# Tables and layer 0's parameter rows loaded in the last piece; ScalarE alone normalizes x; bias rows turned first

## The chip, the core and the metric

The kernel runs on one core of a Trainium2 chip. TensorE (PE), VectorE (DVE), ScalarE (ACT) and GpSimd (POOL) each run a queue of instructions in order; SyncE (SP) issues nearly all DMAs, and POOL issues a few. The metric is the device time of one execution in microseconds (us): the median of 3 runs. A difference of 0.2% (4.6 us) is about what a measurement of this kernel can tell from no change.

## The reference

A trunk of two layers on x, 256 positions by 2048 channels, float32, with a condition vector c. Each layer makes six modulation vectors from c, projects the modulated normalized input into four groups of heads, puts them together, and ends with a gated feed-forward network. The part that the change touches is the start of layer 0:

```python
c_act = jax.nn.silu(c)
mod = (c_act @ w_mod[l] + b_mod[l]).reshape(bn, 6, d)
shift_m, scale_m, gate_m = mod[:, 0, None], mod[:, 1, None], mod[:, 2, None]
h = layer_norm(x) * (1.0 + scale_m) + shift_m
proj = h @ w_in[l]
...
y_b = mla_mixer(..., cos, sin)          # rotary tables
y_d = conformer_conv(ag, conf_w_dw[l], conf_b_dw[l], conf_ln_g[l], conf_ln_b[l])
...
gate = causal_dwconv(gate, w_conv, b_conv)   # in the feed-forward part
```

`w_mod` has 2048 x 12288 numbers a layer (100 MB), so even the two vectors that the first products need, `shift_m` and `scale_m`, take 33.5 MB of weights.

## The kernel before

**Pieces.** Layer 0 cannot wait until all of `shift_m` and `scale_m` is there, so `by_pieces` (L1248) goes through the 2048 input channels in five pieces, `PIECES` (L45): 2, 2, 4, 4 and 4 blocks of 128 channels, called pieces 0 to 4 here. For a piece, `mod_piece` (L251) loads the columns of `w_mod` that make its channels' shift and scale, in units of 1 MB (two DMAs of 512 KB, one for each of the two vectors, tile `wmod`). DVE multiplies each k-block by c's value and adds it up in `qacc` (`mod_step`, L243, its lines L246 and L248). `sums` (L275) lets PE add `qacc` over the partitions (`ps_mod`, L83) on top of the bias, which PE takes from `bcol`, a tile with `b_mod` turned so that channels lie on partitions; ACT writes the result as columns (`mod`, L205 and L86). Then `finish` (L1474) multiplies and shifts the piece's normalized x, `hF`: even blocks on ACT, odd ones on DVE (L1484). From piece 2 on `hF` is also split into a high and a low part, `hT` (L473, L474). PE now adds the piece's share of five groups of products, D, U, V, B and E, into PSUM or into running sums (`sumU` and others, L1280, L1292).

**Order.** A scheduler lays each engine's queue out at build time, and each engine then runs its queue in that order. While piece q is multiplied, the units of piece q+1 are loaded and added up (L1327 to L1342), and `finish` of piece q+1 is called ahead of the last quarter of piece q's D products. SP's queue holds the `wmod` units and the projection's weights (`wexact`, 512 KB or 384 KB; `wraw`, 1 MB, which ACT and DVE split into `whi` L453 and `wlo` L454) interleaved. A transfer can be issued only when its buffer is free: `wmod` and `wraw` share four 1 MB buffers, `wexact` eight buffers of 512 KB. `wmod` buffers are freed by DVE's `qacc` instructions, `wexact` buffers by PE.

**x.** `normed_T` (L1442) loads x's two tiles of 128 positions. DVE takes the statistics (L1449, L569, L571), POOL the power to -0.5 (L114), and DVE the product -mean * rstd (L574). ACT writes the normalized quarter `xn` (L86), PE turns it (`ps_xT`, L1456), and the copy into `hF` goes to ACT for quarters 0 and 2 (L1460) and to DVE for quarters 1 and 3 (L1462).

**Rows.** Small parameters come as rows of 128 numbers and are turned by PE. `load_rows` (L130) lets POOL load them (L135) into one of five buffers and returns a `turn`: a PE transpose (`ps_rows`, L141) and a DVE copy (L142). At the start POOL loads `b_mod` of layer 0, the tables `cst[:, 128:1024]` (rotary tables and small matrices, L157), and the rows of `load_params(0)` (L167): ten DMAs for four turns, `pm` (conformer weights; norms and other small ones) and `pf` (feed-forward convolution, two turns). `turn_b0` stands in `finish` of piece 0 (L1476), the four others in `finish` of piece 1 (L1487 to L1490). POOL then loads the same five sets of rows for layer 1 as soon as the five buffers are free again.

After piece 4, the rest of group B and then C follow (`B_c`, `C_c`), while DVE and ACT work on group D's convolution (`gluD`, `convD`, `prodD`), on A's mixing (`va`, `wT`, `ps_mix`) and on attention (`mix_b`, L1023), which needs the tables, `pm` and `rr` (`ps_ss`, `ps_rkv`, `dgB`).

Of the kernel before, what the change touches and what calls it, by code (L numbers as in the profile page):

```python
# [13 lines left out]
P = 128  # L14
# [40 lines left out]
def encoder_kernel(ctx: ExitStack, tc: tile.TileContext, A: dict, consts: bass.AP, out: bass.AP):  # L55
# [71 lines left out]
    cact = keep.tile([P, 16], F32, name="cact")  # L127
    dve.tensor_copy(cact, pst[:, 0:16])

    def load_rows(parts, n, dst):  # L130

        r = smallp.tile([P, P], F32, tag="rows", name="rows", bufs=5)
        at = 0
        for ap in parts:
            pool.dma_start(out=r[at : at + ap.shape[0], :], in_=ap)  # L135
            at += ap.shape[0]
        assert at == n

        def turn():
            ps = ms_tile("ps_rows")  # L140
            pe.transpose(ps[:, 0:n], r[0:n, :], ident[0:n, 0:n])  # L141
            dve.tensor_copy(dst, ps[:, 0:n])  # L142
# [12 lines left out]
    turn_b0 = load_rows([rows(A["b_mod"][0])], 96, bcol[0])

    pool.dma_start(out=cst[:, 128:1024], in_=consts[:, 128:1024])  # L157

    PM = []
    PF = []  # L160
# [1087 lines left out]
    def by_pieces(l, w_in, hF, between, mix_d, mix_u, mix_v, mix_b, mix_c, mix_e):  # L1248
# [52 lines left out]
        for q, (k0, nkt) in enumerate(PIECES):  # L1301
# [140 lines left out]
    def normed_T(hF):  # L1442
# [3 lines left out]
        for t in range(2):  # L1446
            st = new_stats(f"in{t}")
            for c in range(4):
                dve.bn_stats(out=st[:, c, :], in_=X[t][:, c * 512 : (c + 1) * 512])  # L1449
            r = rstd_of(st, f"in{t}", True)[1]  # L1450
            for q in range(4):
                xn = tmp_tile("xn")
                ident_act(xn, X[t][:, q * 512 : (q + 1) * 512], r[:, 0:1], r[:, 1:2])
                ps = ms_tile("ps_xT")
                for j in range(4):
                    pe.transpose(ps[:, j * P : (j + 1) * P], xn[:, j * P : (j + 1) * P], ident)  # L1456
                dst = hF[q][:, :, t * P : (t + 1) * P]
                src = ps.rearrange("p (j t) -> p j t", j=4)
                if q % 2 == 0:
                    act.copy(dst, src)  # L1460
                else:
                    dve.tensor_copy(dst, src)  # L1462

    def piece(q, hF):

        k0, nkt = PIECES[q]
        units, sums = mod_piece(0, (SHIFT_M, SCALE_M), k0, nkt)
        if q == 0:
            normed_T(hF)
            for u in units:  # L1470
                u()
            turns.extend(load_params(0))

        def finish():  # L1474
            if q == 0:
                turn_b0()  # L1476
            sums()
            for kt in range(k0, k0 + nkt):
                h = hF[kt // 4][:, kt % 4, :]
# [1 line left out]
                if kt % 2 == 0:  # L1481
                    ident_act(h, h, sc, sh)
                else:
                    dve.tensor_scalar(out=h, in0=h, scalar1=sc, scalar2=sh, op0=ALU.mult, op1=ALU.add)  # L1484
            for kt in range(max(k0, PLAIN_KT), k0 + nkt, 2):
                split(hT[kt // 2], hF[kt // 4][:, kt % 4 : kt % 4 + 2, :])
            if q == 1:  # L1487
                for turn in turns:
                    turn()
                turns.clear()  # L1490
# [123 lines left out]
```

## Time and profile before

| what | value |
|---|---|
| runs | 2288.36, 2288.9, 2292.54 us; median 2288.9 us |
| profiled execution | 2287.06 us, its span 2285.3 us |
| PE busy in the span | 2233.5 us (98%) |
| DVE, ACT, POOL busy | 1773.9, 1095.1, 33.7 us |
| DMA | 605.21 MB, mean 265 GB/s |
| granted TensorE clock, mean | 0.991 |

The span runs from the first to the last instruction of the profiled execution; 1.8 us of that execution's time lie around it. Rows of the timeline give the start and the length of a run of like instructions, their engine, line, output and inputs, and in brackets how long the engine sat idle before and what ended that. Rows of the windows give the busy time of PE, its weight loads, DVE, ACT and POOL in a stretch, then the granted clock, the mean busy share of the 16 DMA engines (a saturated stretch reads a little over 1) and GB/s.

### The profile page before, as it was taken

To read this page: it belongs to the slowest core of one execution; us is meant where nothing else is said; L and a number is where in the kernel's file an instruction comes from. 1 tells how busy PE (TensorE), PEld (TensorE's weight loads), DVE (VectorE), ACT (ScalarE), POOL (GpSimd) and SP (SyncE) were. 2 spreads that over 40 slices of the span, in tenths; PEclk is the share of its full clock that TensorE was granted. 3 is DMA by queue.
4 is the path that set the end of the run, shared out by engine and by line. 5 is a ranking of instruction groups with operands and counts; after the bars stand their busy time and mean duration, and the time that the engine had idled before them with its cause. 6 is when DMAs were issued, how large, how long until landed. Compare 5 with 4: busy or idle time off the path is not lost.

```text
span 2285.3 us, 31502 instructions
## 1 busy us (share of the span) xinstructions
PE 2233.5 (98%) x12387; PEld 1929.9 (84%) x12387; DVE 1773.9 (78%) x2187; ACT 1095.1 (48%) x1638; POOL 33.7 (1%) x65
## 2 busy tenths in 40 slices
PE   6999999999999999999999999999999999999998
PEld 4788886798888888888789999889888888888886
DVE  5768988788888888988977899787676565565776
ACT  3346741354455444544454434545544454454553
POOL 1000000000000000000000000000000000000000
PEclk9999999999999999999999999999999999999999
DMA  9999789778888888898767667775666555555554
GB/s 350 371 364 354 276 310 360 249 277 315 310 310 313 314 303 329 301 345 305 276 221 260 197 237 251 275 272 188 239 240 206 200 183 192 195 186 191 187 193 148
DMA packets 228717, 605.21 MB, mean 265 GB/s; under 512 B 14660, under 2 KB 27188, under 8 KB 210900
## 3 DMA queue, kind: packets, MB, share of 16 engines
q1 hardware_dynamic: 227784, 602.30, 74.2%
q8 instruction: 97, 1.59, 0.3%
q0 software_dynamic: 784, 0.90, 0.1%
q14 instruction: 52, 0.43, 0.0%
HBM read 601.05 MB, written 2.10 MB: 264 GB/s over the span
## 4 chain that ended last, share of the span: by engine, by line
PE 53%; DVE 4%; DMA 1%; issue 1%; ACT 1%; POOL 0%; DVEq 0%; POOLq 0%; ACTq 0%
PE d L83 20%; PE v_c L83 12%; PE g_c L83 11%; PE o L83 2%; PE D_c L83 2%; PE C_c L83 2%; PE U_c L83 1%; DVE wlo L454 1%; DVE convD L886 1%; PE E_c L83 1%; DMA wmod<-in_w_mod_dram 1%; DMA wraw<-in_w_out_dram 1%; DVE macc L248 0%; PE ps_mod L83 0%; PE ps_xT L592 0%
## 5 line engine op out<-in xcount | busy, mean ns | idle before, releaser
L453 ACT CAST whi<-wraw 128x1024 fp32r<-128x1024 f32 (+1 forms) x632 | 643.3, 1043 | 750.0 <-PE g_c L83 221.5
L454 DVE TENSOR_TENSOR wlo<-wraw,whi 128x1024 fp32r<-128x1024 f32 (+1 forms) x632 | 750.1, 1214 | 298.9 <-ACT whi L453 276.6
L83 PE MATMUL d<-whi,a 128*128 128x512 f32 x1344 | 390.4, 391 | 0.9 <-ACT whi L453 0.9
L248 DVE SCALAR_TENSOR_TENSOR macc<-wmod,cact,macc 128x2048 f32<-128x2048 f32 (+2 forms) x174 | 353.6, 2033 | 41.3 <-DMA wmod<-in_w_mod_dram 40.7
L83 PE MATMUL v_c<-hT,whi 128*128 128x512 f32 (+1 forms) x1456 | 343.1, 383 | 0.0
L83 PE MATMUL g_c<-hT,whi 128*128 128x512 f32 (+1 forms) x1344 | 313.6, 380 | 1.3 <-DVE second L1429 1.3
L83 PEld LDWEIGHTS v_c<-hT,whi 128*128 128x128 f32 x1456 | 264.5, 189 | 48.5
L83 PEld LDWEIGHTS d<-whi,a 128*128 128x128 f32 x1344 | 253.4, 189 | 54.6 <-ACT whi L453 2.2
L83 PEld LDWEIGHTS g_c<-hT,whi 128*128 128x128 f32 x1344 | 243.4, 189 | 44.9 <-DVE second L1429 1.8
L83 PE MATMUL d<-wlo,a 128*128 128x512 f32 x672 | 235.1, 393 | 1.6 <-DVE wlo L454 1.6
L83 PE MATMUL v_c<-hT,wlo 128*128 128x256 f32 x1400 | 190.7, 283 | 0.0
L83 PEld LDWEIGHTS v_c<-hT,wlo 128*128 128x128 f32 x1400 | 183.1, 191 | 6.6
L83 PE MATMUL g_c<-hT,wlo 128*128 128x256 f32 x1280 | 175.8, 283 | 0.0
L83 PEld LDWEIGHTS g_c<-hT,wlo 128*128 128x128 f32 x1280 | 168.2, 191 | 5.9
L83 PEld LDWEIGHTS d<-wlo,a 128*128 128x128 f32 x672 | 127.1, 189 | 30.2 <-DVE wlo L454 3.8
L473 ACT CAST a<-g 128x512 fp32r<-128x512 f32 x132 | 80.7, 619 | 91.8 <-PE d L83 90.0
L83 PE MATMUL o<-whi,a 128*128 128x512 f32 x384 | 110.1, 392 | 0.5 <-ACT whi L453 0.5
L474 DVE TENSOR_TENSOR a<-g,a 128x512 fp32r<-128x512 f32 x132 | 87.6, 683 | 10.2 <-ACT a L473 10.2
L248 DVE SCALAR_TENSOR_TENSOR qacc<-wmod,cact,qacc 128x1024 f32<-128x1024 f32 (+1 forms) x75 | 80.3, 1070 | 10.5 <-DMA wmod<-in_w_mod_dram 8.4
L83 PEld LDWEIGHTS o<-whi,a 128*128 128x128 f32 x384 | 71.9, 188 | 16.6 <-ACT whi L453 0.9
L83 PE MATMUL D_c<-hT,whi 128*128 128x256 f32 x432 | 83.1, 292 | 2.4 <-ACT hT L473 1.6
L83 PEld LDWEIGHTS D_c<-hT,whi 128*128 128x128 f32 x432 | 69.8, 197 | 4.8 <-ACT hT L473 1.7
(370 smaller groups left out, 2605.9 us busy)
## 6 DMA issues: line engine op xcount, KB each, us to landing
wraw<-in_ffn_w_up_dram SPq DMA_DIRECT2D x168, 1024.0 KB, 5.0
wmod<-in_w_mod_dram SPq DMA_DIRECT2D x134, 1024.0 KB, 6.7
wraw<-in_ffn_w_down_dram SPq DMA_DIRECT2D x88, 1024.0 KB, 5.2
wraw<-in_w_in_dram SPq DMA_DIRECT2D x33, 1024.0 KB, 6.6
wmod<-in_w_mod_dram SPq DMA_DIRECT2D x64, 512.0 KB, 9.5
wraw<-in_w_out_dram SPq DMA_DIRECT2D x26, 1024.0 KB, 6.9
wmod<-in_w_mod_dram SPq DMA_DIRECT2D x32, 768.0 KB, 7.4
wexact<-in_w_in_dram SPq DMA_DIRECT2D x46, 512.0 KB, 8.0
```

Source lines behind the costliest of these rows:

```text
L83: pe.matmul(o, lhsT, rhs, start=start, stop=stop, skip_group_check=True)
L248: i = dve.scalar_tensor_tensor(out=acc, in0=w, scalar=col, in1=acc, op0=ALU.mult, op1=ALU.add)
L453: act.copy(hi[:, :m], r)
L454: i = dve.tensor_tensor(out=lo[:, :m], in0=r, in1=hi[:, :m].bitcast(F32), op=ALU.subtract)
L473: act.copy(hi, src)
L474: dve.tensor_tensor(out=lo, in0=src, in1=hi.bitcast(F32), op=ALU.subtract)
L886: dve.scalar_tensor_tensor(out=yd[:, j, 30 - k :], in0=glu[:, j, : S - 30 + k], scalar=CW(k, j), in1=yd[:, j, 30 - k :], op0=ALU.mult, op1 ...
```

## The change

Four things are edited.

1. `turn_b0` moves from `finish` of piece 0 to a place ahead of `normed_T`: `b_mod`'s rows are turned first.
2. `normed_T` no longer uses `rstd_of`. DVE writes var + eps and -mean; POOL takes the power; ACT makes -mean * rstd by a Copy of -mean with rstd as its scale. All eight turned quarters are copied into `hF` by ACT.
3. The tables' DMA and the rows of `load_params(0)` are issued in `finish` of piece 4, with a dependency (a semaphore) on the last DVE instruction that modulates `hF` there.
4. Their four turns are called during piece 4's products: one after V, one after E, two after the last quarter of D. The `next(mods)` calls there are as before.

```diff
     turn_b0 = load_rows([rows(A["b_mod"][0])], 96, bcol[0])
-
-    pool.dma_start(out=cst[:, 128:1024], in_=consts[:, 128:1024])
...
-                if k0 + nkt == KT and s < 3:
-                    next(mods)
+                if k0 + nkt == KT:
+                    if s < 3:
+                        next(mods)
+                    if s > 0:
+                        turns.pop(0)()
+                    if s == 3:
+                        turns.pop(0)()
...
-            r = rstd_of(st, f"in{t}", True)[1]
+            mv = smallp.tile([P, 2], F32, tag="mv", name=f"mv_in{t}", bufs=4)
+            dve.bn_aggr(out=mv, in_=st)
+            r = smallp.tile([P, 3], F32, tag="rin", name=f"r_in{t}")
+            dve.tensor_scalar(out=r[:, 0:1], in0=mv[:, 1:2], scalar1=LN_EPS, scalar2=None, op0=ALU.add)
+            dve.tensor_scalar(out=r[:, 2:3], in0=mv[:, 0:1], scalar1=-1.0, scalar2=None, op0=ALU.mult)
+            power(r[:, 0:1], r[:, 0:1])
+            act.activation(out=r[:, 1:2], in_=r[:, 2:3], func=AF.Copy, scale=r[:, 0:1])
...
-                dst = hF[q][:, :, t * P : (t + 1) * P]
-                src = ps.rearrange("p (j t) -> p j t", j=4)
-                if q % 2 == 0:
-                    act.copy(dst, src)
-                else:
-                    dve.tensor_copy(dst, src)
+                act.copy(hF[q][:, :, t * P : (t + 1) * P], ps.rearrange("p (j t) -> p j t", j=4))
...
         if q == 0:
+            turn_b0()
             normed_T(hF)
             for u in units:
                 u()
-            turns.extend(load_params(0))
...
-                    dve.tensor_scalar(out=h, in0=h, scalar1=sc, scalar2=sh, op0=ALU.mult, op1=ALU.add)
+                    i = dve.tensor_scalar(out=h, in0=h, scalar1=sc, scalar2=sh, op0=ALU.mult, op1=ALU.add)
+            if q + 1 == len(PIECES):
+                d = pool.dma_start(out=cst[:, 128:1024], in_=consts[:, 128:1024])
+                tc.add_manual_dep(d.ins, i.ins.name, data_dep, reason="the pieces' weights go first")
+                turns.extend(load_params(0, i))
```

(`load_params` and `load_rows` pass the instruction on and add the same dependency to each row DMA.)

DVE's queue at the start of layer 0, before: `st_in`, `mv_in` and `rs_in` are the norms' small columns, `qacc` piece 0's sums, `hF` the turned x.

```order
L571 TENSOR_SCALAR rs_in1_187<-mv_in1_185 128x1
L246 TENSOR_SCALAR qacc_134<-wmod_223,cact_104 128x512
L248 SCALAR_TENSOR_TENSOR qacc_134<-wmod_223,cact_104,qacc_134 128x512 x2
L574 SCALAR_TENSOR_TENSOR rs_in0_144<-mv_in0_142,rs_in0_144 128x1
L574 SCALAR_TENSOR_TENSOR rs_in1_187<-mv_in1_185,rs_in1_187 128x1
L248 SCALAR_TENSOR_TENSOR qacc_134<-wmod_223,cact_104,qacc_134 128x512
L248 SCALAR_TENSOR_TENSOR qacc_134<-wmod_230,cact_104,qacc_134 128x512 x3
L1462 COPY hF1_116<-ps_xT_158 128x4x128
L248 SCALAR_TENSOR_TENSOR qacc_134<-wmod_230,cact_104,qacc_134 128x512
L1462 COPY hF3_118<-ps_xT_174 128x4x128
L248 SCALAR_TENSOR_TENSOR qacc_134<-wmod_237,cact_104,qacc_134 128x512
L1462 COPY hF1_116<-ps_xT_201 128x4x128
```

The same place with the change (`bcol` is the turned bias, `r_in` the norm's columns):

```order
L144 COPY bcol0_106<-ps_rows_134 128x96
L1456 BN_STATS st_in0_139<-x0_97 128x6 x4
L1458 BN_AGGR mv_in0_144<-st_in0_139 128x2
L1460 TENSOR_SCALAR r_in0_146<-mv_in0_144 128x1
L1461 TENSOR_SCALAR r_in0_146<-mv_in0_144 128x1
L1456 BN_STATS st_in1_183<-x1_98 128x6 x4
L1458 BN_AGGR mv_in1_188<-st_in1_183 128x2
L1460 TENSOR_SCALAR r_in1_190<-mv_in1_188 128x1
L1461 TENSOR_SCALAR r_in1_190<-mv_in1_188 128x1
L248 TENSOR_SCALAR qacc_133<-wmod_227,cact_104 128x512
L250 SCALAR_TENSOR_TENSOR qacc_133<-wmod_227,cact_104,qacc_133 128x512 x3
L250 SCALAR_TENSOR_TENSOR qacc_133<-wmod_234,cact_104,qacc_133 128x512 x4
```

The four copies into `hF` and the two products for the norm are gone from between the sums, the copy of the bias (before, four `qacc` ahead of the end of piece 0's sums) stands ahead of x's statistics, and piece 0's sixteen `qacc` instructions stand in one run.

DVE's queue in the products of piece 4, before (`wlo`: low parts of weights, `macc`: sums for a later modulation vector, `gluD`: the first step behind group D, `wT`: A's mixing weights, turned):

```order
L474 TENSOR_TENSOR hT<-hF_118,hT 128x2x256 x2
L246 TENSOR_SCALAR macc<-wmod,cact 128x2048
L454 TENSOR_TENSOR wlo<-wraw,whi 128x1024 x3
L248 SCALAR_TENSOR_TENSOR macc<-wmod,cact,macc 128x2048
L454 TENSOR_TENSOR wlo<-wraw,whi 128x1024 x4
L248 SCALAR_TENSOR_TENSOR macc<-wmod,cact,macc 128x2048
L454 TENSOR_TENSOR wlo<-wraw,whi 128x1024
L248 SCALAR_TENSOR_TENSOR macc<-wmod,cact,macc 128x2048 x2
L875 TENSOR_TENSOR gluD<-D_c_119,sg 128x512
L875 TENSOR_TENSOR gluD<-D_c_120,sg 128x512
L987 COPY wT<-ps_wT 128x512
```

And with the change (`pm`, `pf`: the turned parameters):

```order
L456 TENSOR_TENSOR wlo<-wraw,whi 128x1024 x3
L250 SCALAR_TENSOR_TENSOR macc<-wmod,cact,macc 128x2048
L456 TENSOR_TENSOR wlo<-wraw,whi 128x1024 x4
L144 COPY pm_110<-ps_rows 128x124
L456 TENSOR_TENSOR wlo<-wraw,whi 128x1024
L250 SCALAR_TENSOR_TENSOR macc<-wmod,cact,macc 128x2048 x2
L144 COPY pm_110<-ps_rows 128x29
L250 SCALAR_TENSOR_TENSOR macc<-wmod,cact,macc 128x2048
L144 COPY pf_111<-ps_rows 128x128
L144 COPY pf_111<-ps_rows 128x48
L877 TENSOR_TENSOR gluD<-D_c_118,sg 128x512
L877 TENSOR_TENSOR gluD<-D_c_119,sg 128x512
```

The four copies, which stood in piece 2's `qacc` run before, are now here, two of them right ahead of `gluD`, and one `macc` has gone back behind a `wlo`.

POOL's queue around the two powers, before (`rows_260` and `rows_262` are the last two of layer 0's row sets, `rows_2737` the first of layer 1's):

```order
L135 DMA rows_260<-in_ffn_w_conv_dram 128x128
L135 DMA rows_262<-in_ffn_w_conv_dram 4x128
L135 DMA rows_262<-in_ffn_b_conv_dram 44x128
L114 ISA
L114 TENSOR_TENSOR rs_in0_144<-rs_in0_144,mhalf_93 128x1
L114 TENSOR_TENSOR rs_in1_187<-rs_in1_187,mhalf_93 128x1
L135 DMA rows_2737<-in_b_mod_dram 96x128
```

And with the change (`rows_108` is layer 0's bias, `cst` the tables, `rows_1021` and `rows_1023` the first of layer 0's other sets):

```order
L135 DMA rows_108<-in_b_mod_dram 96x128
L104 MEMSET flat_84 128x1 x4
L114 ISA
L114 TENSOR_TENSOR r_in0_146<-r_in0_146,mhalf_93 128x1
L114 TENSOR_TENSOR r_in1_190<-r_in1_190,mhalf_93 128x1
L1492 DMA cst_82<-in_consts_dram 128x896
L135 DMA rows_1021<-in_conf_w_dw_dram 124x128
L135 DMA rows_1023<-in_mla_q_norm_dram 3x128
```

The powers stand ahead of the tables and of all rows but the bias; layer 1's loads follow behind layer 0's, ahead of the clearing of `wT` as before.

More of the change, by code (lines that the diff above doesn't have):

```diff
@@ L128, in encoder_kernel, with load_rows @@
     dve.tensor_copy(cact, pst[:, 0:16])
-    def load_rows(parts, n, dst):
+    def load_rows(parts, n, dst, behind=None):
         r = smallp.tile([P, P], F32, tag="rows", name="rows", bufs=5)
@@ L134, in load_rows @@
         for ap in parts:
-            pool.dma_start(out=r[at : at + ap.shape[0], :], in_=ap)
+            i = pool.dma_start(out=r[at : at + ap.shape[0], :], in_=ap)
+            if behind is not None:
+                tc.add_manual_dep(i.ins, behind.ins.name, data_dep, reason="the pieces' weights go first")
             at += ap.shape[0]
@@ L149, in rows @@
         return ap.rearrange("k (j p) -> (k j) p", p=P)
+    order_dep = mybir.DependencyInfo(mybir.DependencyClass.NoSync, mybir.DependencyReason.DATA)
+    data_dep = mybir.DependencyInfo(mybir.DependencyClass.Sync, mybir.DependencyReason.DATA)
     bcol = []
@@ L165, in encoder_kernel, with load_params @@
         PF.append(pf)
-    def load_params(l):
+    def load_params(l, behind=None):
         turns = []
         if l > 0:
-            turns.append(load_rows([rows(A["b_mod"][l])], 96, bcol[l]))
-        turns.append(load_rows([rows(A["conf_w_dw"][l])], 124, PM[l][:, 0:124]))
+            turns.append(load_rows([rows(A["b_mod"][l])], 96, bcol[l], behind))
+        turns.append(load_rows([rows(A["conf_w_dw"][l])], 124, PM[l][:, 0:124], behind))
         turns.append(
@@ L183, in load_params @@
                 PM[l][:, 124:153],
+                behind,
             )
@@ L186, in load_params @@
         wc = rows(A["ffn_w_conv"][l])
-        turns.append(load_rows([wc[0:128]], 128, PF[l][:, 0:128]))
-        turns.append(load_rows([wc[128:132], rows(A["ffn_b_conv"][l])], 48, PF[l][:, 128:176]))
+        turns.append(load_rows([wc[0:128]], 128, PF[l][:, 0:128], behind))
+        turns.append(load_rows([wc[128:132], rows(A["ffn_b_conv"][l])], 48, PF[l][:, 128:176], behind))
         return turns
     MOD, MOD_BY = {}, {}
-    order_dep = mybir.DependencyInfo(mybir.DependencyClass.NoSync, mybir.DependencyReason.DATA)
-    data_dep = mybir.DependencyInfo(mybir.DependencyClass.Sync, mybir.DependencyReason.DATA)
     def mod_cols(l, m, k0, acc):
@@ L1471, in piece @@
                 u()
-            turns.extend(load_params(0))
         def finish():
-            if q == 0:
-                turn_b0()
             sums()
@@ L1483, in finish @@
                 else:
-                    dve.tensor_scalar(out=h, in0=h, scalar1=sc, scalar2=sh, op0=ALU.mult, op1=ALU.add)
+                    i = dve.tensor_scalar(out=h, in0=h, scalar1=sc, scalar2=sh, op0=ALU.mult, op1=ALU.add)
[3 more added lines that the diff above has]
+                turns.extend(load_params(0, i))
             for kt in range(max(k0, PLAIN_KT), k0 + nkt, 2):
                 split(hT[kt // 2], hF[kt // 4][:, kt % 4 : kt % 4 + 2, :])
[L1487 to L1490, printed above, removed]
         return ([] if q == 0 else units), finish
```

## The prediction

> **What bounds the kernel now.** I read the head of the page first: what the span holds, and whose work fills it.
>
> ```profile
> span 2285.3 us, 31502 instructions
> PE 2233.5 (98%) x12387; PEld 1929.9 (84%) x12387; DVE 1773.9 (78%) x2187; ACT 1095.1 (48%) x1638; POOL 33.7 (1%) x65
> ```
>
> PE does 2233.5 us of 2285.3. What the change can save lies in the other 52 us, most of it at the start, and it is kept only if what feeds PE later can follow. So I cut the start into stretches (columns: stretch, its length, busy PE, PEld, DVE, ACT, POOL, granted clock, DMA share, GB/s).
>
> ```profile
> 5.00:22.00 17.00, 3.95 (x17) 3.26 (x18) 12.09 (x23) 5.23 (x8) 4.22 (x8) 1.00 1.06 364
> 22.00:40.00 18.00, 13.25 (x59) 11.01 (x58) 14.95 (x23) 3.68 (x8) 0.59 (x1) 0.81 1.08 362
> 40.00:58.00 18.00, 18.00 (x82) 14.20 (x80) 6.19 (x10) 7.09 (x14) 0.00 (x0) 1.00 1.05 390
> 58.00:62.00 4.00, 4.00 (x19) 3.31 (x19) 3.96 (x7) 0.10 (x1) 3.77 (x8) 1.00 0.54 145
> 62.00:70.00 8.00, 7.98 (x39) 6.73 (x38) 7.79 (x7) 1.59 (x3) 1.31 (x3) 1.00 1.02 366
> 70.00:130.00 60.00, 56.91 (x296) 46.83 (x297) 43.31 (x42) 26.18 (x46) 0.00 (x0) 0.94 1.04 391
> ```
>
> The transfers are saturated (share over 1) from 5 to 130 us but for one hole, 58 to 62 (0.54, 145 GB/s). PE idles until about 33 us and is full behind that but for small gaps. Two limits therefore lie over each other: when PE can begin, and when bytes arrive. The timelines of PE and DVE show the first, and where the two meet.
>
> ```profile
> 7.28 2.47 DVE L1449 BATCH_NORM_STATS2 st_in<-x 128x6 f32<-128x512 f32 x4 [2.46 <-DMA x<-in_x_dram]
> 11.36 2.47 DVE L1449 BATCH_NORM_STATS2 st_in<-x 128x6 f32<-128x512 f32 x4 [1.12 <-DMA x<-in_x_dram]
> 14.61 0.49 DVE L246 TENSOR_SCALAR qacc<-wmod,cact 128x512 f32<-128x512 f32 x1 [0.29 <-DMA wmod<-in_w_mod_dram]
> 27.16 3.11 DVE L248 SCALAR_TENSOR_TENSOR qacc<-wmod,cact,qacc 128x512 f32<-128x512 f32 x4
> 33.18 5.16 PE L83 MATMUL D_c<-hF,wexact 128*128 128x256 f32 x16
> 55.85 0.95 PE L83 MATMUL ps_mod<-onesR,qacc 128*128 128x1 f32 x8
> 57.13 0.41 DVE L1484 TENSOR_SCALAR hF<-hF,mod,mod 128x256 f32<-128x256 f32 x1 [5.45 <-ACT mod L86]
> 70.38 3.67 PE L83 MATMUL V<-wexact,hF 128*128 128x512 f32 x8 [0.39 <-DMA wexact<-in_w_in_dram]
> ```
>
> Piece 0's sums end on DVE at 30.27 (27.16 + 3.11); 2.9 us later (reduction on PE, `mod`, `hF`) D starts, at 33.18. From there PE runs to 70.38, where V of piece 1 waits 0.39 us for its weights. That is the first place where PE catches up with the transfers: a gain at the start has to pass it.
>
> **The start, on the engines.** What one instruction costs, by the groups of the first 33 us (count | busy us, mean ns | idle before):
>
> ```profile
> L248 DVE SCALAR_TENSOR_TENSOR qacc<-wmod,cact,qacc 128x512 f32<-128x512 f32 x15 | 11.2, 748 | 0.8 <-DMA wmod<-in_w_mod_dram 0.5
> L86 ACT ACTIVATE xn<-x,rs_in 128x512 f32<-128x512 f32 x8 | 6.1, 809 | 12.5 <-DVE rs_in L574 12.5
> L1462 DVE COPY hF<-ps_xT 128x512 f32<-128x512 f32 x4 | 2.8, 688 | 0.8 <-PE ps_xT L1456 0.8
> L1460 ACT COPY hF<-ps_xT 128x512 f32<-128x512 f32 x4 | 2.3, 575 | 0.8 <-PE ps_xT L1456 0.8
> L142 DVE COPY bcol<-ps_rows 128x96 f32<-128x96 f32 x1 | 0.2, 250 | 0.0
> ```
>
> Sixteen sums take 0.49 + 15 x 0.748 = 11.7 us; before, they took 14.61 to 30.27 = 15.7, with 2.8 of copies, 0.25 of `bcol` and two short products among them. Now they stand in one run, and two bounds hold. By DVE: x's second tile should land some 1.4 us sooner, since the tables and rows (0.63 MB at 364 GB/s are 1.7 us) no longer share its transfer time; DVE starts the sums at 13.2 and ends at 24.9. By bytes: behind the first x tile (7.28) come 1 MB of x and eight transfers of 0.52 MB, 5.2 MB or 14.4 us at 364 GB/s, so the last unit is in at 21.7 to 22; four sums behind it (3.0) end at 24.7 to 25. Both say 25.0: 5.3 us sooner, D at 27.9.
>
> ACT now does 8 x (0.809 + 0.575) = 11.1 us, two tiny products besides. From the first norm (7.28 + 2.47 of statistics, short columns and POOL's power: about 11) and with a wait for the second tile it ends at 22 to 23.5. PE needs these columns at 27.9, ACT itself is wanted for `mod` at about 26: the cover is 2.5 us or more, so the move costs nothing; with a cover gone each further 1.4 us of ACT would count in full. The bias turn on PE and its 0.25 us copy now stand ahead of x on DVE; DVE was idle there for 2.46 us, so nothing.
>
> **What leaves the boundary of piece 2.** The four turns stand between D products there:
>
> ```profile
> 57.60 0.44 PE L141 MATMUL ps_rows<-cst,rows 124*128 124x124 f32 x2
> 58.51 0.47 PE L141 MATMUL ps_rows<-cst,rows 128*128 128x128 f32 x2
> SPq L263 <- DVE pf L142: 9.0, 1, 9.0
> ```
>
> PE gets back 0.8 us (0.44 + 0.47, less overlap), and is 6.1 us ahead. The last row is from SP's waits: one `wmod` issue stood 9.0 us until DVE had come past its modulation of piece 1 (57.13) and the turns' copies; that made the hole. With DVE let through at about 52, buffers come free at about 53 to 54, before the earlier issues run out (at 58, or 56 with fewer bytes ahead): the hole should close.
>
> **How far the transfers follow.** Ahead of V's weights no longer come the tables 0.46, layer 0's rows 0.17 and, while piece 0 runs, layer 1's `b_mod` 0.05 MB: 0.68 MB / 0.363 = 1.9 us. The hole gives (390 - 145) x 4 us = 0.98 MB, 2.5 us. Layer 1's rows, in 62 to 70 us: (391 - 366) x 8 = 0.2 MB, 0.5 us. Together 4.9 us. So PE, 6.1 ahead, waits 1.2 us more at V than before and goes on 4.9 ahead; behind that the transfers stay at 1.04, so no more comes until 130 us. The 0.8 of the turns and some of the start are lost in this wait.
>
> **Piece 4.** POOL loads once DVE has modulated there:
>
> ```profile
> 158.18 0.74 DVE L1484 TENSOR_SCALAR hF<-hF,mod,mod 128x256 f32<-128x256 f32 x2 [0.86 <-ACT mod L86]
> 177.54 0.40 PE L83 MATMUL D_c<-hT,whi 128*128 128x256 f32 x2
> rows<-in_conf_w_dw_dram POOLq DMA_DIRECT2D x2, 62.0 KB, 5.3
> 140.00:185.00 45.00, 45.00 (x293) 39.67 (x292) 29.38 (x25) 25.96 (x37) 0.00 (x0) 1.00 0.92 328
> 4.32 0.50 POOL L135 DMA_DIRECT2D rows<-in_sconv_w_dram  x1
> 59.75 0.50 POOL L135 DMA_DIRECT2D rows<-in_sconv_w_dram  x1
> ```
>
> DVE's second modulation ends at 158.9, now 154.0. The tables and ten row loads at 0.5 us are issued by 160, and rows land 5.3 us later, by 166. The first turn stands behind V, at 177.54, now 172.6; the others later: no wait, 6 us and more of cover. On PE the turns cost again 0.8 us, as at their old place: 4.9 - 0.8 = 4.1.
>
> On DVE the four copies cost about 1.1 us; two come right ahead of `gluD`, in a stretch that this view of DVE shows:
>
> ```profile
> 188.58 2.35 DVE L248 SCALAR_TENSOR_TENSOR macc<-wmod,cact,macc 128x2048 f32<-128x2048 f32 x1 [4.40 <-DMA wmod<-in_w_mod_dram]
> 190.84 1.28 DVE L875 TENSOR_TENSOR gluD<-D_c,sg 128x512 f32<-128x512 f32 x2
> 204.19 1.10 DVE L1009 TENSOR_TENSOR mixed<-ps_mix,gmlp 128x256 f32<-128x256 f32 x3 [0.59 <-PE ps_mix L83]
> 226.12 1.70 PE L83 MATMUL ps_ss<-onesR,sqB 128*128 128x1 f32 x12 [0.98 <-ACT sqB L1045]
> 235.34 0.67 PE L83 MATMUL ps_rkv<-dgB,onesR 128*128 128x256 f32 x2 [0.76 <-DVE dgB L1074]
> ```
>
> DVE waits 4.40 us for the last `macc`; the first two copies go into such idle. The last two delay `gluD` by some 0.65, and 0.59 of idle at 204.19 takes most of that back. PE waits for this chain at 226.12 and 235.34, 1.74 us in all: bounds of this term are +0.8 (all copies arrive there) and -1.7 (both waits go, since the new order has a `convD` step less ahead of `dgB`'s column). I take +0.1 (0.65 - 0.59), the rows nearest to `gluD`. The 0.63 MB beside the weights of piece 4 cost nothing: from 140 to 185 us, 328 GB/s run where 391 is full, room for 2.8 MB. Without it they would put off that last `macc` by 1.6 us (0.63 / 0.391), which `gluD` would feel.
>
> **Sum.** -4.9 + 0.8 + 0.1 = -4.0. The profiled span 2285.3 becomes 2281.3, its execution 2287.06 becomes 2283.1. That execution lies 1.8 us below the median of the runs, 2288.9; I carry the difference over to the median: 2284.9.
>
> **The rivals.** One measurement of this kernel tells 0.2%, 4.6 us, from no change: faster is below 2284.3. The forecast stands at the edge of it.
>
> *A, the forecast*: -4.0, 2284.9; chance 0.45.
>
> *B, the hole stays*: `wmod` buffers come free late after all, since the sums of piece 1 wait for their own units. Then bytes give 2.4, less 0.9: -1.5, 2287.4. Against it: DVE idled 5.45 us ahead of 57.13, so it was done with those sums. Chance 0.12.
>
> *C, the longer stall at V turns the clock down.* PE waits 1.6 us there where it waited 0.39. Other waits of that length, and the clock in a stretch behind them:
>
> ```profile
> 87.00 0.98 PE L83 MATMUL D_c<-hT,whi 128*128 128x256 f32 x4 [1.62 <-ACT hT L473]
> 93.00:94.00 1.00, 1.00 (x7) 1.00 (x7) 1.00 (x1) 0.00 (x0) 0.00 (x0) 0.50 1.06 391
> 226.00:228.00 2.00, 1.88 (x13) 1.88 (x14) 2.00 (x4) 1.57 (x5) 0.00 (x0) 0.82 0.99 416
> 228.00:230.00 2.00, 2.00 (x6) 1.55 (x6) 2.00 (x3) 2.00 (x7) 0.00 (x0) 0.50 1.01 418
> ```
>
> After 1.62 us of idle at 87 and 0.98 at 226 the granted clock was 0.50. Half a clock over about 3.4 us (an estimate: 228 to 230 is wholly at 0.50, 226 to 228 at 0.82 holds 0.7 us of it, and as much again is taken for the far edge) loses 1.7: -2.3, 2286.6. Chance 0.18. [...]
>
> *D, more than forecast*: the waits of 226.12 and 235.34 go, up to 1.74, and with the first the half clock behind it, 1.7: -5.7 to -7.4 if all goes, -4.0 if nothing; I put it at -6.0, 2282.9. For it: the shorter DVE order ahead of `dgB`. Against: two copies more ahead of `gluD`. Chance 0.20.
>
> *E, the slower side: POOL's issues drag in piece 4.* If an issue takes long while DVE is busy, the last turn's rows come too late, and PE, which runs in order, stands at the turn with C's and B's products queued behind it. From 154.0 to the last turn (about 184, an estimate between the end of V, 172.6, and `gluD`, 190.84 - 4.9) less 5.3 of landing are 25 us for 11 issues: it decides from 2.3 us an issue. [...] Against it: an issue took 0.50 us at 59.75, where DVE was 99% busy, as at 4.32. [...] Chance 0.05.
>
> **How the numbers follow.** C, B and A's upper bounds (+0.8 for `gluD`, +1.6 for a late `macc`) reach to 2287.4, and the highest cases together with some of the runs' own spread to 2288.6; D and the lower bounds reach to 2280.8, which leaves out E and part of D's far end. Faster by over 0.2%: D and nearly half of A, 0.41; slower: E, 0.05; within: the rest, 0.54.
>
> **What would show it.** Right: D of piece 0 at 27.9; DVE's sums from 13.2 to 25.0 without a gap of note; ACT's last copy before 25; no stretch near 58 under 350 GB/s; a wait of 1 to 2 us at V of piece 1; no wait at any of the four turns; the end of V in piece 4 4.9 us earlier, the last product 4.0. Wrong: D begins after 29 (ACT, or bytes); V does not wait and PE is 6 ahead at 87; half clock behind V (C); PE idle at a turn (E).

## The result and the profile after

| | before | with the change |
|---|---|---|
| median of 22 runs each | 2289.44 us | 2284.57 us |
| lowest to highest | 2285.3 to 2293.68 | 2278.27 to 2288.76 |
| ratio to before | | 0.9981 (95%: 0.9974 to 0.9989) |
| profiled execution, span | 2287.06, 2285.3 | 2281.42, 2279.7 |

The kernel became 4.9 us faster by the medians and some 4.3 by the ratio, whose interval is 2.5 to 6.0 us: about the 0.2% (4.6 us) that a single comparison tells from nothing, and with 22 runs of each not nothing. Much of the spread goes with the clock: each run's mean granted clock is on record beside its time, and of the change's 22 runs the four at 0.987 took 2286.6 to 2287.0 us, while three of the four at 0.993 or above took 2278.3 to 2279.0.

The stretches of the kernel after, as they were shown of before (busy PE, PEld, DVE, ACT, POOL, granted clock, DMA share, GB/s):

```profile
5.00:22.00 17.00, 9.22 (x35) 6.58 (x35) 14.53 (x27) 10.40 (x18) 1.35 (x2) 1.00 1.07 371
22.00:40.00 18.00, 15.14 (x55) 13.09 (x56) 13.11 (x20) 2.19 (x5) 0.00 (x0) 1.00 1.08 365
40.00:58.00 18.00, 18.00 (x83) 14.49 (x82) 7.24 (x9) 6.02 (x12) 0.00 (x0) 1.00 1.03 376
58.00:62.00 4.00, 4.00 (x20) 3.54 (x19) 3.89 (x4) 0.00 (x0) 0.00 (x0) 1.00 1.03 355
62.00:70.00 8.00, 7.52 (x27) 4.53 (x26) 7.61 (x7) 3.88 (x7) 0.00 (x0) 1.00 1.03 376
70.00:130.00 60.00, 57.30 (x315) 49.03 (x314) 43.77 (x41) 23.98 (x42) 0.00 (x0) 0.94 1.04 389
```

The hole at 58 to 62 us is filled, 355 GB/s for 145; a little of it has gone to the stretch before, 376 for 390. ScalarE now carries the first stretch (10.40 for 5.23). The marks of the timeline, DVE and ACT first:

```profile
13.57 11.78 DVE L250 SCALAR_TENSOR_TENSOR qacc<-wmod,cact,qacc 128x512 f32<-128x512 f32 x15
21.39 0.58 ACT L1470 COPY hF<-ps_xT 128x512 f32<-128x512 f32 x1 [0.60 <-PE ps_xT L1469]
28.26 6.53 PE L83 MATMUL D_c<-hF,wexact 128*128 128x256 f32 x16
65.94 3.67 PE L83 MATMUL V<-wexact,hF 128*128 128x512 f32 x8 [0.48 <-DMA wexact<-in_w_in_dram]
82.56 1.23 PE L83 MATMUL D_c<-hT,whi 128*128 128x256 f32 x4 [1.62 <-ACT hT L475]
```

Piece 0's sums are one run that ends at 25.35; ScalarE is done at 21.97; D starts at 28.26, 4.9 us sooner than before. But D's first 16 products take 6.53 us, where they took 5.16, and V of piece 1 waits only 0.48 us and starts 4.4 us sooner.

In piece 4, the first and the slowest of POOL's issues, and PE's turns:

```profile
154.50 0.61 POOL L1492 DMA_DIRECT2D cst<-in_consts_dram  x1 [140.56 <-DVE hF L1490]
156.66 1.40 POOL L135 DMA_DIRECT2D rows<-in_sconv_w_dram  x1
172.83 0.27 PE L143 MATMUL ps_rows<-cst,rows 124*128 124x124 f32 x1
181.66 0.24 PE L143 MATMUL ps_rows<-cst,rows 29*128 29x29 f32 x1
184.81 0.46 PE L143 MATMUL ps_rows<-cst,rows 128*128 128x128 f32 x2
```

The issues begin at 154.50 and one of them took 1.40 us where the others take 0.5 to 0.6; no turn has an idle time ahead of it. Further on, where attention begins, the waits of 0.98 and 0.76 us are 0.29 and none, but the clock was low for longer:

```profile
220.82 1.94 PE L83 MATMUL ps_ss<-onesR,sqB 128*128 128x1 f32 x12 [0.29 <-ACT sqB L1047]
231.66 0.59 PE L83 MATMUL ps_rkv<-dgB,onesR 128*128 128x256 f32 x2
222.00:226.00 4.00, 4.00 (x12) 3.37 (x13) 4.00 (x7) 3.82 (x10) 0.00 (x0) 0.50 1.01 425
226.00:230.00 4.00, 4.00 (x14) 3.28 (x14) 3.71 (x9) 4.00 (x12) 1.01 (x1) 0.68 1.00 411
```

How far PE is ahead along the run I read as its **lead**: the start of a product in the kernel before less that of the same product in this one, as the median over all products that start in a stretch of before's time. It is 3.55 us at 40 to 54, 4.44 at 71 to 79, 4.72 at 140 to 170, 3.75 behind the turns (196 to 218), 2.28 at 430 to 480, and 5.61 at 2000 to 2200.

### The profile page after: what moved, and what is told of

Read it like the earlier page. It is cut to its first block, busy times and chain, and to the rows that moved or that the text cites. A ratio compares the mean times of both kernels' runs of the same rounds, so it can differ in the third digit from the quotient of the medians.

```text
span 2279.7 us, 31503 instructions
## 1 busy us (share of the span) xinstructions
PE 2238.7 (98%) x12387; PEld 1934.8 (85%) x12387; DVE 1773.3 (78%) x2183; ACT 1098.2 (48%) x1644; POOL 35.1 (2%) x65
## 4 chain that ended last, share of the span: by engine, by line
PE 88%; DVE 7%; DMA 2%; ACT 2%; issue 1%; POOL 0%; SPq 0%; DVEq 0%; ACTq 0%; POOLq 0%
PE g_c L83 22%; PE v_c L83 22%; PE d L83 20%; PE o L83 7%; PE D_c L83 3%; PE C_c L83 3%; PE B_c L83 2%; PE U_c L83 1%; PE E L83 1%; PE E_c L83 1%; DVE wlo L456 1%; PE ps_mod L83 1%; PE V L83 1%; DVE qacc L250 1%; DVE macc L250 1%
```

## The experiments

Two theories were open behind the result. Theory 1: the bytes ahead of V's weights of piece 1 decide how much of the gain is kept. Theory 2: those weights are issued behind VectorE's first sums of piece 2, so they follow the engines, whatever the bytes. All kernels are the whole change with edits; each ratio is to the kernel before in the same session. "First D, lead" is that of the first product, "V, lead" that of V's first product of piece 1, the other two are the medians over 140 to 170 and 196 to 218 us.

| kernel | first D, lead | 16 D, us | wait at V | V, lead | lead 140-170 | lead 196-218 | ratio (95%) |
|---|---|---|---|---|---|---|---|
| before | 0 | 5.16 | 0.39 | 0 | 0 | 0 | |
| the change | 4.9 | 6.53 | 0.48 | 4.4 | 4.7 | 3.8 | 0.9981 (0.9974 to 0.9989) |
| the change again | 5.1 | 5.81 | 0.29 | 5.5 | 5.4 | 3.3 | 0.9985 (0.9976 to 0.9993) |
| start only | 2.5 | 5.31 | 0.47 | 2.3 | 2.7 | 2.7 | 1.0002 (0.9990 to 1.0014) |
| moved only | 1.2 | 6.63 | 0.56 | 0.5 | 0.1 | -0.9 | 0.9997 (0.9985 to 1.0008) |
| copies on VectorE | 1.4 | 6.69 | 0.34 | 0.9 | 0.1 | -0.9 | 1.0000 (0.9988 to 1.0012) |
| tables behind piece 0 | 5.3 | 6.07 | 1.30 | 4.5 | 5.2 | 4.2 | 0.9989 (0.9979 to 0.9999) |
| idle products | 6.1 | 5.18 | 1.91 | 5.5 | 6.2 | 5.2 | 0.9974 (0.9958 to 0.9991) |
| idle products, tables behind piece 0 | 6.2 | 6.70 | 1.44 | 4.6 | 5.2 | 4.2 | 1.0001 (0.9992 to 1.0009) |
| V's weights earlier | 5.0 | 5.73 | none | 6.0 | 5.9 | 4.9 | 0.9987 (0.9976 to 0.9998) |
| turns at the start | 5.2 | 6.57 | 0.24 | 4.9 | 5.7 | 5.7 | 0.9969 (0.9959 to 0.9979) |
| turns at the start, V earlier | 4.7 | 5.41 | none | 6.0 | 5.3 | 5.3 | 0.9973 (0.9959 to 0.9987) |
| turns at the start, idle products | 3.6 | 5.41 | 0.11 | 4.6 | 5.3 | 4.6 | 0.9995 (0.9985 to 1.0005) |
| all three | 1.7 | 5.41 | none | 3.0 | 4.6 | 4.6 | 0.9990 (0.9981 to 1.0000) |

The wait at V was ended by the weights' transfer, but in the repeat by ScalarE's `sumU`. Copies on VectorE, idle products, turns at the start, and turns at the start with V earlier were run in one session on another chip than the other experiments; the change itself was not timed in that session. With 6 to 12 runs each the intervals are some 2 to 4 us to each side, so they settle few single terms; the leads do. One thing in the expectations is to be read otherwise: they give -3.75 as the change's mark at the turning of A's weights (`ps_wT`). That is the lead of the products around it; the turning itself has another place in PE's queue with the change, 187.89 for 189.05. I read the column 196 to 218 in its stead.

**The start only.** Tables, rows and turns stand as before (rows issued in `piece(0)`, turned in `finish` of piece 1); the bias turn and ScalarE's work are the change's.

```diff
+    pool.dma_start(out=cst[:, 128:1024], in_=consts[:, 128:1024])
...
+            turns.extend(load_params(0))
...
```

> Only the start is changed (bias turned first, ScalarE alone on x); tables and rows load at the start and are turned at piece 2's boundary, as before. Marks are given against the kernel before: first D of piece 0, start of V of piece 1, turning of A's weights (ps_wT). The whole change has -4.9, -4.4, -3.75 there. Theory 1 (bytes ahead of V's weights set V): D -3.5, since x's second tile and the last unit come as late as before; V no better than -2.5, what the closed hole gives; ps_wT the same -2.5, since no turns cost PE in piece 4; time -2.5. Theory 2 (V's weights follow the engines: they are issued behind VectorE's first sums of piece 2): D -3.5, V -3.5, ps_wT -3.5, time -3.5.

DVE's timeline there:

```profile
10.98 2.47 DVE L1453 BATCH_NORM_STATS2 st_in<-x 128x6 f32<-128x512 f32 x4 [1.01 <-DMA x<-in_x_dram]
17.93 9.41 DVE L251 SCALAR_TENSOR_TENSOR qacc<-wmod,cact,qacc 128x512 f32<-128x512 f32 x12 [0.81 <-DMA wmod<-in_w_mod_dram]
```

DVE waits again for x's second tile (1.01) and for a unit (0.81); the sums end at 27.34, D leads by 2.5 and not 3.5. V leads by 2.3 with a short wait, so this run does not tell the theories apart. The lead of 2.7 is kept past piece 4, with no turns there; the time shows no gain (0.9990 to 1.0014).

**The moves only.** VectorE keeps the norm's product and half of the copies, and the bias turn its old place in `finish` of piece 0.

```diff
+            r = rstd_of(st, f"in{t}", True)[1]
...
+                if q % 2 == 0:
+                    act.copy(dst, src)
+                else:
+                    dve.tensor_copy(dst, src)
...
-            turn_b0()
...
+            if q == 0:
+                turn_b0()
```

> Only tables and rows are moved and turned in piece 4; VectorE keeps four copies of x and the bias copy among its sums. Both theories: D of piece 0 -1.4 (x and the units land sooner, the 15.7 us of VectorE's run stay), V of piece 1 -2.2 without a longer wait (the turns' 0.8 are gone), ps_wT -1.3 with the turns' 0.9 paid back; time -1.3. If V came at -4 or earlier here, the bytes alone would make the gain and the start's edit nothing.

D leads by 1.2, near the 1.4 expected, but its 16 products took 6.63 us, 1.5 more than before. So V led by 0.5 and not by 2.2, and PE passed 140 us with no lead and paid 1.0 for the turns behind that. The slow clock is no accident of one profile here: over its 11 runs this kernel's mean granted clock is 0.9875, that of the kernel before in the session 0.9901 (and with the copies on VectorE, the next kernel, 0.9875 for 0.9894). The time shows nothing either way.

**Copies on VectorE.** Of the whole change only the copies of the odd quarters are undone.

```diff
+                if q % 2 == 0:
+                    act.copy(dst, src)
+                else:
+                    dve.tensor_copy(dst, src)
```

> The whole change, but VectorE copies the odd quarters of x again. My term: four copies of 0.69 us stand in VectorE's run of sums, which bounds D: D of piece 0 at -4.9 + 2.8 = -2.1, V of piece 1 at -2.9 without a wait, ps_wT -2.0. Rival (the last unit's transfer bounds the sums): D stays within 0.5 us of -4.9.

```profile
13.68 0.69 DVE L1475 COPY hF<-ps_xT 128x512 f32<-128x512 f32 x1 [0.96 <-PE ps_xT L1469]
19.68 0.69 DVE L1475 COPY hF<-ps_xT 128x512 f32<-128x512 f32 x1 [0.64 <-PE ps_xT L1469]
20.29 8.62 DVE L250 SCALAR_TENSOR_TENSOR qacc<-wmod,cact,qacc 128x512 f32<-128x512 f32 x11
```

The sums end at 28.91, 3.6 us later than with the change: the four copies are 2.8 by their own times and 2.4 of the queue's, DVE, which runs in order, stood 0.96 and 0.64 us ahead of two of them for PE, and x came 0.4 us sooner in this execution. So the copies, not the early bias, are what the start gains by. The two halves need each other: alone they lead by 2.7 and 0.1 at 140 to 170 us, together by 4.7 to 5.4. The 0.1 holds 1.5 us of slow clock in D: with the loads moved and copies on VectorE the clock was at half for 17.07 us from 20.8 on, in both profiles (why is not shown). At the first D the leads are 2.5 and 1.2 alone and 4.9 to 5.1 together.

**The change again.** No edit: a second profile, and the time once more.

> The whole change once more, unaltered: how far one execution's marks differ from another's. In its first profile D's 16 products took 6.53 us and V of piece 1 came at -4.44 against the kernel before. If both move with the phase of the clock, D takes between 5 and 6.6 us here, V comes between -4.4 and -5.5, and only the 1.0 us of the turns in piece 4 is the same to 0.1. If the marks are fixed by the order of the queues, they agree to 0.2 us.

```profile
188.30 0.66 PE L988 MATMUL ps_wT<-cst,gmlp 128*128 128x128 f32 x4 [0.90 <-DVE pf L144]
230.81 0.67 PE L83 MATMUL ps_rkv<-dgB,onesR 128*128 128x256 f32 x2 [1.84 <-DVE dgB L1076]
```

D took 5.81 us here and V leads by 5.5, where it was 4.4: the marks do move between executions of one kernel. Here the copies of `pf` made PE wait 0.90 us ahead of A's weights and attention's waits were longer than before the change. The lead at 2000 to 2200 us is 1.13, against 5.61 in the first profile. So a span of one profile says little about a change of this size, and the first profile's 5.6 us is no confirmation of 4.9.

**Tables behind piece 0.** Their 0.46 MB pass ahead of V's weights, but leave the front alone.

```diff
-            if q + 1 == len(PIECES):
+            if q == 0:
                 d = pool.dma_start(out=cst[:, 128:1024], in_=consts[:, 128:1024])
```

> The whole change, but the tables (0.46 MB) are issued once piece 0 is modulated, so that they pass ahead of V's weights of piece 1 without touching the start. D -4.9 in both. Theory 1 (bytes): V's weights come 0.46 MB / 0.37 = 1.2 us later, V at -3.2 with a wait of 1.7 us in place of 0.48, ps_wT -2.5. Theory 2 (engines and issue): V stays at -4.4, ps_wT -3.75.

```profile
65.90 3.67 PE L83 MATMUL V<-wexact,hF 128*128 128x512 f32 x8 [1.30 <-DMA wexact<-in_w_in_dram]
```

V leads by 4.5, as theory 2 has it, but it waits 1.30 us for its weights, as theory 1 has it. Against the change's first profile no time is lost; PE was earlier by 0.9 at 40 us here, and that is what the wait took. These marks leave it undecided, and are the reason for the next two.

**Idle products.** Ten products of the identity with itself (20 records in the trace), behind x's last quarter, ahead of D.

```diff
...
+            warm = acc_tile("warm")
+            for j in range(10):
+                i = pe.matmul(warm[:, 0:128], ident, ident, start=True, stop=True, skip_group_check=True)
+                tc.add_manual_dep(i.ins, last_T[0].ins.name, order_dep, reason="behind x's last quarter")
```

> The whole change with ten idle products of 128x128 on PE behind x's last quarter, into a bank that nobody reads. In the whole change's profile PE idles 2.79 us there, and the first 16 products of D then took 6.53 us where the kernel before has 5.16. If idle time ahead of D is what leaves the clock low, D's 16 products take 3.6 to 5.2 us. Then theory 1 (bytes): V of piece 1 stays at -4.4 to -4.9 and waits 1.5 to 3 us. Theory 2 (engines): V moves with PE to -5.8 or better. If the sums' small products between leave the clock low as well, D takes 5 to 6.5 us as now and nothing moves.

PE's timeline, and the stretch with V:

```profile
27.08 5.18 PE L83 MATMUL D_c<-hF,wexact 128*128 128x256 f32 x16 [0.21 <-ACT hF L86]
64.84 3.67 PE L83 MATMUL V<-wexact,hF 128*128 128x512 f32 x8 [1.91 <-DMA wexact<-in_w_in_dram]
58.00:70.00 12.00, 10.08 (x38) 6.63 (x37) 10.14 (x8) 4.70 (x8) 0.00 (x0) 1.00 1.05 388
```

D starts at 27.08 and takes 5.18 us: PE now leads by 6.1, the amount that the prediction had. The clock was not held up through D: by its record it fell to half at 26.6 for 3.41 us, and D's first products still stand 0.43 us apart. What came sooner is the sums' own products (`ps_mod` from `qacc`, 1.05 us for 1.87 with the change) and x itself (0.4 us sooner in this execution). And with the same ten products in the next kernel D took 6.70 us, so 5.18 is in part luck. V waits 1.91 us and leads by 5.5, between what theory 1 (4.4 to 4.9) and theory 2 (5.8) gave.

**Idle products, tables behind piece 0.** Both edits.

> The whole change with the ten idle products ahead of D, and the tables issued once piece 0 is modulated. PE and with it VectorE's sums are early, so the issue of V's weights is not what holds them. Theory 1 (bytes): V of piece 1 at -5.5 + 1.2 = -4.3 with a wait of about 3 us, and -3 at 200 us. Theory 2 (engines and issue): V at -5.5 with a wait of about 1.9 us, as with the idle products alone.

```profile
65.81 3.67 PE L83 MATMUL V<-wexact,hF 128*128 128x512 f32 x8 [1.44 <-DMA wexact<-in_w_in_dram]
```

V leads by 4.6 with the tables ahead of it and by 5.5 without: 1.0 us for 0.46 MB, which at 388 GB/s are 1.2. Twice with the tables V came at 65.8 to 65.9, with a wait, though PE's lead of 4.4 and 4.6 at 40 us would have let it come sooner by theory 2. That is theory 1. (By time the kernel has lost the whole gain, 1.0001 beside 0.9985 for the change in the same session, more than this 1.0 us; the intervals touch, and the trace up to 200 us does not show the rest.) But the change's first profile, without the tables, is no better, 65.94: there the bytes were not the limit. SyncE's waits for `wmod` buffers at 45 to 70 us tell why, of the change first and then of the idle products:

```profile
SPq L265 <- DVE qacc L250: 10.3, 4, 6.3
```

```profile
SPq L265 <- DVE qacc L250: 7.0, 3, 4.2
```

In the change's first profile, with D slow, VectorE modulated piece 1 late, the issue stood 6.3 us, and some of the hole was left (376 GB/s at 40 to 58 us; 390 with the idle products). The issue of V's first weights shows both limits, of the change, its repeat, the tables behind piece 0 and the idle products:

```profile
58.79 0.46 SPq L433 DMA_DIRECT2D wexact<-in_w_in_dram  x1
57.91 0.46 SPq L433 DMA_DIRECT2D wexact<-in_w_in_dram  x1
57.93 0.46 SPq L433 DMA_DIRECT2D wexact<-in_w_in_dram  x1
56.26 0.46 SPq L433 DMA_DIRECT2D wexact<-in_w_in_dram  x1
```

V starts at 65.94, 64.86, 65.90 and 64.84. The second and the third were issued at the same time, and with 0.46 MB more ahead V came 1.04 us later: bytes. The first was issued 0.9 us behind the second, and V came 1.08 later: issue. From the issue to V's start are 6.95 to 7.2 us in the profiles of the kernel before, the change, its repeat, the start only, the moves only and the copies on VectorE, and 8.0 to 8.6 in the other five that keep the order of the loads. So both hold, each where it comes last: in this order of loads V's weights came with a lead of 5.5 at most (bytes), and else some 7 us behind their issue, which waits for VectorE's `qacc`. PE's own lead grows by 1.0 from 40 us to V, since the turns are gone from there: 3.55 and 4.44 in the first profile, 4.43 and 5.52 in the second.

**V's weights earlier.** One unit of piece 2 goes behind them.

```diff
-                some_mods((0.3, 0.7, 1.0, 1.0)[s])
+                some_mods((0.3, 0.55 if q == 1 else 0.7, 1.0, 1.0)[s])
```

> The whole change, but the queue of SyncE has V's weights of piece 1 ahead of one more unit of piece 2 (1 MB, 2.7 us). The wait of 0.48 us at V goes. If nothing else waits for that unit, V starts at -4.9, ps_wT at -4.2, and the time is 0.5 us below the whole change. Rival: piece 2's last sums come later with that unit and PE waits as much more at D of piece 2: ps_wT -3.75 as with the whole change.

```profile
68.51 5.69 PE L83 MATMUL B<-hF,wexact 128*128 128x256 f32 x24 [0.52 <-DMA wexact<-in_w_in_dram]
82.12 1.60 PE L83 MATMUL D_c<-hT,whi 128*128 128x256 f32 x5 [2.05 <-ACT hT L475]
```

V does not wait and leads by 6.0, but B now waits 0.52 and D of piece 2 2.05 for 1.62. The lead at 140 to 170 us is 5.9, above the change's 4.7 and 5.4; the time cannot show it.

**Turns at the start.** Layer 0's rows load in front, PE turns them while it is idle, ScalarE copies them (`act.copy` in the turn); tables and layer 1's rows load in piece 4.

```diff
+            for turn in load_params(0, "start"):
+                turn()
             normed_T(hF)
...
-                    if s > 0:
-                        turns.pop(0)()
-                    if s == 3:
-                        turns.pop(0)()
```

> The whole change, but layer 0's rows (0.17 MB) load at the start and are turned there, while PE is idle, and ScalarE copies them; the tables still load in piece 4, and layer 1's rows wait for the same instruction as there. PE then has no turns in piece 4. My term: the turns cost PE 0.8 to 1.0 us in piece 4, so ps_wT comes at -4.3 to -4.7 against the kernel before (the whole change -3.75), if V of piece 1 is at -4.0 to -4.4 (0.17 MB more ahead of it are up to 0.45 us). Rival: the rows hold up x or ScalarE at the start, D of piece 0 comes later than -4.4, and nothing is won.

The lead is 5.65 at 140 to 170 us and 5.66 at 196 to 218: the turns' 1.0 us is gone. Of the eight profiles with the turns in piece 4, seven lost 0.96 to 0.99 between these two stretches (the repeat lost 2.1, with its 0.90 of waiting); of the five without them, four lost nothing and one 0.70 (turns at the start, idle products; 0.25 of it is a wait ahead of `ps_mix`). The rows did not hold up D (5.2), but they used up the cover: ScalarE begins x at 15.70, for 11.23 with the change, and its last copy ends at 25.65, 0.1 us behind the sums. This is the fastest by ratio, 0.9969; it beats the kernel before, but its interval overlaps that of the change, which was timed in other sessions, and the trace accounts for about 1 us between the two. Part of the ratio is the clock: these ten runs have a mean granted clock of 0.9909, the kernel before in the same session 0.9894.

**Turns at the start, V earlier.**

> Two edits together on the whole change: rows loaded and turned at the start with ScalarE's copies, and V's weights of piece 1 ahead of one more unit. If the two terms add up (0.9 us of turns, 0.5 us of wait), ps_wT comes at -4.7 to -5.2 against the kernel before, and the time is 1 to 1.5 us below that of the whole change, which five rounds may not tell apart; the marks of the trace do. Rival: the wait only moves to D of piece 2, and ps_wT is -4.3.

V leads by 6.0 without a wait, and the lead is 5.3 at 140 us: B waits 1.42 us for its weights, and the half us did not add up. The rival was right that the wait only moves; it went to B, not to D of piece 2.

**Turns at the start, idle products**, and **all three.**

> The whole change with layer 0's rows loaded and turned at the start (no turns in piece 4) and the ten idle products ahead of D. If the two gains add up, D's 16 products take about 5.2 us, V of piece 1 comes at -5.0 to -5.5 (where the bytes hold it), and PE stays there past piece 4: -5.5 to -6.2 at 200 us against the kernel before, where the whole change has -3.75; time 1.5 to 2.5 us below the whole change. Rival: the bytes of the rows hold V at -4.9, and the idle products bring nothing: -5.6 at 200 us, as without them.

> As the one before, and V's weights of piece 1 stand ahead of one more unit. If V's weights are what holds PE there, the wait at V goes and PE is at -6 or better at 100 us and at 200 us. Rival: the wait goes over to D of piece 2, whose last sums wait for the unit that now comes behind V's weights: -5.3 to -5.6 at 200 us, no better than without the edit.

Both fell short: at 196 to 218 us they lead by 4.6, where 5.5 to 6.2 and 6 were expected. PE's timeline of the first:

```profile
24.95 2.40 PE L1484 MATMUL warm<-cst 128*128 128x128 f32 x20
29.57 5.41 PE L83 MATMUL D_c<-hF,wexact 128*128 128x256 f32 x16 [0.25 <-ACT hF L86]
```

ScalarE takes up x only at 15.76 here, as with the turns at the start alone, because the row copies and the second tile's norm stand ahead of it in its queue. x's last quarter is then turned at 24.5, and the ten products, free in the idle time of the other kernel, stand in PE's way: D starts at 29.57, and at 31.50 with all three, where they took 3.55 us and not 2.40. What is free to add at a place is so only as long as that place is idle.

## Why the prediction came out right, and where its steps did not

**The start: right.** The sums ran from 13.06 to 25.35 (13.2 to 25.0 forecast), ScalarE was done at 21.97 (before 25), D started at 28.26, in the repeat 28.09 (27.9). The cover of ScalarE was real. What I had not seen is that this cover and the copies are most of the gain: without them D leads by 1.4.

**The lead at V: wrong in the making, right in the amount.** The step said: PE comes to V 6.1 us ahead, the bytes allow 4.9, the rest is waited away, 1.6 us in all. PE came 4.5 ahead, since D's first products ran slow, and waited 0.48. V led by 4.4 and, in the repeat, by 5.5; that the forecast lies between is luck, since two errors went against each other. The bytes allow 5.5, as the idle products show, so that term was 0.6 too small; and its premise, that the bytes come last, holds only where D is quick. The step that failed is PE's own lead behind D's start: it took D's 5.16 us over from before, and the clock in it moves from one execution to the next (6.53 and 5.81 with the change).

**The hole: right, but for a rest.** It closed to 355 GB/s (over 350 was forecast), though 6.3 us of the issue's 9.0 are still waited in the first profile and 5.7 in the repeat. The rest goes with V's weights coming 1.1 us later in the first profile (65.94) than with the idle products (64.84).

**The turns in piece 4: right, a little small.** 0.97 for 0.8, the same in seven profiles; no turn waited for its rows, so rival E did not come: it decides from 2.3 us an issue, and the slowest that a run shows took 1.52. An issue that takes long beside VectorE's work is there all the same, 1.40 us with the change. VectorE's row beside it (156.66 to 158.06) is

```profile
156.68 1.28 DVE L248 TENSOR_SCALAR macc<-wmod,cact 128x2048 f32<-128x2048 f32 x1
```

In all twelve profiles that issue rows in piece 4, just one issue took over 1 us (1.39 to 1.52 us), it is the one under this instruction, whichever rows it loads, and it ends 0.1 us behind it. The other issues, beside VectorE's instructions with two tensor inputs (`wlo`, `hT`, `macc` from `macc`), took 0.5 to 0.6 us. So busy alone does not tell: the 0.50 us at 59.75, which the prediction set against the rival, stood beside `qacc` instructions, with two. (The slow issue is also the fifth of its row each time, but among those of the kernel before at 58 to 63 us none is slow; the instruction was not moved to try it.) Here it cost nothing, since 25 us were to spare.

**Attention: too small, and not by rival D's way.** +0.1 was forecast. The waits went nearly away in the first profile, as rival D had it, and the lead stayed 3.75 on both sides of that stretch, since the clock was halved for twice as long (6.83 us from 221.71 on, for 3.41 from 227.26 on before). In the repeat the waits came back, 0.30 and 1.84 us, with a lead of 4.5 behind them. All the profiles together tell more. The wait ahead of `ps_ss` is 0.29 or 0.30 in all eight with the turns in piece 4 and 0.98 or 0.99 in the six without; that ahead of `ps_rkv` is 1.84 or 1.85 in six of the eight, and 0.74 to 0.76 in four of the six. So the new order takes 0.7 from the first wait and adds 1.1 to the second: +0.4 us in all. The second wait is 0.16 us or none in the three profiles (the change's first, the idle products, turns at the start) whose half clock begins by 222 us and slows PE ahead of it; so its going goes with the clock, not with the order.

**Rival C: refuted.** A wait of 1.91 us at V (idle products) left the clock at 1.00 from 58 to 70 us. V's eight products took 3.67 us, as with the change, so no unrecorded half clock hides there. My reading of 87 and 226 us, that 1 to 1.6 us of idle time halves the clock, was wrong (and at 87 us the half clock lasted 6.83 us by its record, not the 3.4 that I took). What those two places have and V has not is shown by the rows ahead of D of piece 2 with the change, where the record goes to half at 81.76:

```profile
78.36 1.84 PE L83 MATMUL ps_mod<-onesR,qacc 128*128 128x1 f32 x16
80.06 0.88 PE L83 MATMUL ps_mod<-bcol,cst 128*128 128x4 f32 x4
```

2.6 us of products with one to four columns come right before the 1.62 us of idle time, and at 226 us stand `ps_ss` products of one column, 1.70 us of them from 226.12 on, with the half clock from 227.26. Whether such products have to do with the clock was not tried, so what halves it at these places is not shown.

**The sum.** 4.0 forecast, 4.9 measured by the medians (2.5 to 6.0 by the interval of the ratio). Behind 240 us nothing of the change is at work, yet the lead of the two profiles goes from 3.8 to 5.6 and from 4.5 to 1.1; the medians over 22 runs average over that. So the traces show a lead of 3.8 to 4.5 us behind attention; what the medians have above that rests on the medians alone.

## What to carry to other kernels

Where two limits lie over each other, an edit against one of them can show much less by itself than beside the other: the moved loads and ScalarE's copies were worth 1.2 and 2.5 us of lead at the first D alone and 4.9 to 5.1 together, and neither showed in the time alone. Follow a gain from mark to mark (first product, next place that waits for a transfer, behind the last added work) and compare one mark in several executions before a term is made of it. And work that is free because an engine idles there is not free any more once something else delays the place.

## What the runs showed of the hardware

D's and U's products of 128x256 start 0.43 us apart at a granted clock of 0.50 and 0.22 at 1.00 (the kernel before, up to 35.9 us and from 36.4 on). Where the clock changes is not fixed by the kernel alone: D's first 16 took 6.53 and 5.81 us in the two profiles of the change, and 5.16 to 6.70 over the profiles of all kernels. By the record of the granted clock, its half lasts 6.83, 6.83, 3.41, 6.83, 6.83 and 3.41 us in the profile of the kernel before and 6.83, 6.83, 3.41, 6.83, 3.41, 3.41 and 3.41 in the change's first (the last of each, 8.63 and 8.55 us at its end, left out), 13.65 in the repeat (18.7 to 32.3 us), 3.41 with the idle products (from 26.6 us on), and 17.07 with the moves only and with the copies on VectorE (from 20.8 us on): in all of these a multiple of 3.41.

The granted clock can be missing at the start of a profile: its record begins at 33.97 us in the change's first and at 22.46 in that of the kernel before. Of the change's first profile, and then of the repeat:

```profile
30.00:34.00 4.00, 4.00 (x11) 3.10 (x11) 3.76 (x5) 0.00 (x0) 0.00 (x0) 1.00 1.09 359
34.00:36.00 2.00, 2.00 (x11) 1.77 (x10) 1.20 (x2) 0.00 (x0) 0.00 (x0) 1.00 1.05 369
```

```profile
26.00:30.00 4.00, 3.96 (x15) 3.50 (x15) 2.46 (x5) 1.02 (x3) 0.00 (x0) 0.50 1.10 355
```

Both read 1.00 in the first, yet 11 products take 4 us (D's stand 0.43 us apart up to 33.96) and then 11 take 2 (0.22 apart); the repeat has 0.50 recorded over 26 to 30 us, at the same place in the kernel. Where the first stretches of a profile read 1.00, the products' own times are the better witness.
